# A written order for ScalarE, VectorE and GpSimd in the memory and attention stage, shorter steps in its chains, and rotations on VectorE

## The chip, the cores and the metric

The kernel runs on one core of a Trainium2 chip. The engines of the core are TensorE (PE in the rows, with PEld for its weight loads), VectorE (DVE), ScalarE (ACT), GpSimd (POOL) and SyncE (SP), whose queue issues the transfers. The metric is the device time of one execution in microseconds; lower is better. A change of less than 0.2% is about what a measurement of this kernel cannot tell from none.

## The reference

One encoder layer: 512 tokens of 2048 channels, float32. A combined projection feeds four mixers of 512 channels each; their outputs are normed, concatenated and projected back; cross attention on 256 memory tokens and a mixture of 32 experts follow. Cut to what the changed stage computes:

```python
z = rms_norm(h, norm_mix) @ w_in                  # columns split into za, zb, zc, zd
# A, diff_attention(za): 4 heads, two softmax maps of 64 channels each
q, k = apply_rope(q, cos, sin), apply_rope(k, cos, sin)
lam = exp(sum(lf[0] * lf[1])) - exp(sum(lf[2] * lf[3])) + lam_init
sc = einsum('bhcqd,bhckd->bhcqk', q, k) * scale
p = softmax(sc); attn = p[:, :, 0] - lam * p[:, :, 1]
o = rms_norm(attn @ v, subln_g) * (1 - lam_init)
# C, dilated_attention(zc): 4 heads of 128 channels, rope, keys in three strided windows
# D, s5_bidir(zd): complex linear recurrence over the sequence, both directions,
y = C x + d_skip * u;  gl = gelu(y);  od = rms_norm(gl * sigmoid(gl @ glu_w + glu_b))
h = h + concat(oa, ob, oc, od) @ w_out
# cross attention: keys and values of the memory, 4 heads of 512 channels
k, v = split(rms_norm(mem) @ wkv);  p = softmax((rms_norm(h) @ wq) k^T);  h = h + (p v) @ wo
def apply_rope(x, cos, sin):
    x1, x2 = split(x)
    return concat([x1 * cos - x2 * sin, x2 * cos + x1 * sin])
```

## The kernel before

The kernel is a sequence of stages on one instruction stream per engine. **The stage of the change** runs from about 737 to 1335 us. TensorE has one steady load there, a list of *units* (class `Units`), and two *chains* are laid into it.

The units are the memory's part of cross attention, which needs no token yet (`cross_fold`). `project` makes 128 channels of the memory's keys or values, `keys` multiplies keys by a strip of `xa_wq`, and `values` multiplies values by a strip of `xa_wo`. Every float32 product is made of three float32r products of a high and a low part (`mm3`; `split` makes the parts: the high one is a cast on ScalarE, the low one a subtraction on VectorE). So each half of a weight tile, `wraw` from memory, becomes `whi` by ScalarE and `wlo` by VectorE before TensorE can use it. `Units.get` keeps at most three halves split ahead of TensorE (`NB = 4`). A half feeds 12 matmuls of 256 columns, or 6 of 512. The names in the rows: `mh`, `ml` are the memory's parts, `kvz`, `kvh`, `kvl` a projected strip and its parts, `kvo` an output strip, `pj` the accumulators.

The chains are Python generators: `s5()` (mixer D: `s5_states`, `s5_outputs`, `s5_gate`) and `attention()` (four heads of `diff_head`, four of `dil_head`, then `norm_512`). A `yield x` says that the chain's next piece should come x microseconds of modelled TensorE time later, and `Units.step` emits pieces of units until then (x is stretched by `SLACK`: 1.5 for attention, 1.43 for s5). When the units have run out, the chain's pieces follow each other directly.

A head begins in `head_inputs`: `rope_load` fetches q and k (`at_q`, `at_k`) and copies of them with swapped halves (`at_qr`, `at_kr`), `rope` multiplies each by a table, adds the two (`at_full`) and splits the sum (`at_qh`, `at_ql`). Then come the transposition of v, and four tiles of 128 queries, each with scores (`mm3`), softmax, and a transposition one tile later.

On TensorE the order of the code is kept in this stage. On ScalarE, VectorE and GpSimd a scheduler orders the instructions, with a raised priority for the splits (`high_priority(HP)`). Each engine runs its list strictly in order, and so does each DMA queue. In the rows the program's `s5_` is written `s_`, and numbers at the end of names are left out.

## Time and profile before

| | us |
|---|---|
| runs of the kernel | 2723.89, 2726.25, 2730.3 (median 2726.25) |
| the profiled execution | 2721.49 |
| its span in the trace | 2719.8 |
| TensorE busy over the span | 2610.1 (96%) |
| VectorE, ScalarE, GpSimd busy | 1344.8 (49%), 927.9 (34%), 239.7 (9%) |

The profiled execution's time is the span and 1.7 us around it, and it lies 4.8 us below the median of the runs. TensorE is busy nearly throughout, so the rows to look for are the few in which it stands idle, with the engine that released it in brackets.

### The profile page before, as it was taken

To read this page: it belongs to the slowest core of one execution; us is meant where nothing else is said; L and a number is where in the kernel's file an instruction comes from. 1 tells how busy PE (TensorE), PEld (TensorE's weight loads), DVE (VectorE), ACT (ScalarE), POOL (GpSimd) and SP (SyncE) were. 2 spreads that over 40 slices of the span, in tenths; PEclk is the share of its full clock that TensorE was granted. 3 is DMA by queue.
4 is the path that set the end of the run, shared out by engine and by line. 5 is a ranking of instruction groups with operands and counts; after the bars stand their busy time and mean duration, and the time that the engine had idled before them with its cause. 6 is when DMAs were issued, how large, how long until landed. Compare 5 with 4: busy or idle time off the path is not lost. (4 is left out here: it accounts for less than half of the span.)

```text
span 2719.8 us, 43651 instructions
## 1 busy us (share of the span) xinstructions
PE 2610.1 (96%) x17976; PEld 1796.1 (66%) x17976; DVE 1344.8 (49%) x2407; ACT 927.9 (34%) x1695; POOL 239.7 (9%) x373
## 2 busy tenths in 40 slices
PE   8899999999979889999999999899999999999996
PEld 6787777777768778869788878644444444444432
DVE  6747474737387654566533344443334433333322
ACT  5134243443256554555533334321111111111103
POOL 0400000000024950000000000000000000000002
PEclk9999999999989989999999999899999999999999
DMA  7432121222266657756633352399999999999997
GB/s 253 163 130 69 57 75 53 88 66 72 95 173 180 200 178 217 231 178 189 229 120 121 98 186 70 152 379 423 423 423 422 425 420 424 426 424 425 421 427 305
DMA packets 156668, 639.96 MB, mean 235 GB/s; under 512 B 25264, under 2 KB 58672, under 8 KB 131376
## 3 DMA queue, kind: packets, MB, share of 16 engines
q1 hardware_dynamic: 156464, 637.12, 62.7%
q8 instruction: 143, 2.34, 0.3%
q14 instruction: 61, 0.50, 0.1%
HBM read 597.75 MB, written 39.32 MB: 234 GB/s over the span
## 5 line engine op out<-in xcount | busy, mean ns | idle before, releaser
L1035 DVE TENSOR_TENSOR wlo<-wraw,whi 128x512 fp32r<-128x512 f32 x556 | 396.1, 720 | 380.5 <-ACT whi L1034 372.2
L1034 ACT CAST whi<-wraw 128x512 fp32r<-128x512 f32 x556 | 339.4, 620 | 555.8 <-PE pj L159 480.4
L159 PE MATMUL ph<-wch,mo_xT 128*64 128x512 f32 x2048 | 455.0, 596 | 5.0 <-DMA wch<-in_moe_w_dram 4.9
L159 PEld LDWEIGHTS ph<-wch,mo_xT 128*64 128x64 f32 x2048 | 140.9, 137 | 277.2 <-issue 263.6
L159 PE MATMUL pj<-xh,whi 128*128 128x512 f32 x688 | 292.8, 426 | 7.0 <-ACT xh L1037 6.6
L159 PE MATMUL pj<-xh,wlo 128*128 128x512 f32 x688 | 272.0, 395 | 7.4 <-DVE wlo L1035 7.4
L159 PE MATMUL pj<-xl,whi 128*128 128x512 f32 x688 | 271.6, 395 | 0.0
L159 PE MATMUL py<-wch,mo_h 128*64 128x512 f32 (+1 forms) x1040 | 231.2, 591 | 2.0 <-ACT mo_h L2108 1.4
L2117 DVE TENSOR_TENSOR mo_A<-ps,mo_A 128x512 f32<-128x512 f32 (+1 forms) x260 | 163.6, 676 | 131.2 <-PE ps L2116 131.2
L1035 DVE TENSOR_TENSOR mo_lo<-H,mo_hi 128x512 fp32r<-128x512 f32 x128 | 87.8, 687 | 171.7 <-ACT mo_hi L1034 171.6
L159 PE MATMUL pj<-mh,whi 128*128 128x256 f32 x512 | 151.7, 296 | 19.3 <-ACT mh L1037 14.7
L159 PEld LDWEIGHTS pj<-xh,whi 128*128 128x128 f32 x688 | 130.4, 190 | 47.2 <-issue 10.3
L1034 ACT CAST mo_hi<-H 128x512 fp32r<-128x512 f32 x128 | 79.1, 619 | 239.5 <-PE ps L159 239.5
L159 PEld LDWEIGHTS py<-wch,mo_h 128*64 128x64 f32 x1040 | 70.7, 136 | 134.1 <-issue 115.5
L159 PEld LDWEIGHTS pj<-xh,wlo 128*128 128x128 f32 x688 | 130.4, 190 | 38.0 <-DVE wlo L1035 9.6
L159 PEld LDWEIGHTS pj<-xl,whi 128*128 128x128 f32 x688 | 130.6, 190 | 26.9 <-issue 3.1
L159 PE MATMUL pj<-mh,wlo 128*128 128x256 f32 x512 | 146.8, 287 | 0.8 <-DVE wlo L1035 0.7
L159 PE MATMUL pj<-ml,whi 128*128 128x256 f32 x512 | 146.8, 287 | 0.1
L159 PE MATMUL ps<-mo_OH,mo_hi 128*128 128x256 f32 x512 | 134.6, 299 | 5.7 <-DVE mo_OH L1997 4.8
L1037 ACT ACTIVATE mo_yh<-py,mo_g 128x512 fp32r<-128x512 f32 (+1 forms) x65 | 44.3, 681 | 246.8 <-PE py L159 246.8
L159 PE MATMUL ps<-mo_OH,mo_lo 128*128 128x256 f32 x512 | 128.3, 286 | 0.0
L159 PEld LDWEIGHTS ps<-mo_OH,mo_hi 128*128 128x128 f32 x512 | 98.9, 193 | 33.5 <-issue 32.6
(507 smaller groups left out, 4698.1 us busy)
## 6 DMA issues: line engine op xcount, KB each, us to landing
wch<-in_moe_w_dram SPq DMA_DIRECT2D x191, 2048.0 KB, 12.4
wraw<-in_w_in_dram SPq DMA_DIRECT2D x85, 512.0 KB, 3.9
wraw<-in_xa_wkv_dram SPq DMA_DIRECT2D x64, 512.0 KB, 4.6
wraw<-in_xa_wq_dram SPq DMA_DIRECT2D x32, 512.0 KB, 4.1
wraw<-in_xa_wo_dram SPq DMA_DIRECT2D x32, 512.0 KB, 4.4
wraw<-in_w_out_dram SPq DMA_DIRECT2D x32, 512.0 KB, 4.2
Ad<-kvo SPq DMA_DIRECT2D x32, 256.0 KB, 3.2
VWd<-kvo SPq DMA_DIRECT2D x32, 256.0 KB, 4.4
```

Source lines behind the costliest of these rows:

```text
L159: nc.tensor.matmul(out, lhsT, rhs, start=start, stop=stop)
L1034: nc.scalar.copy(hi, x)
L1035: nc.vector.tensor_tensor(lo, x, hi.bitcast(F32), op=OP.subtract)
L1037: nc.scalar.activation(hi, x, AF.Copy, scale=scale)
L2117: nc.vector.tensor_tensor(A[:, t, c:c + n], pc, A[:, t, c:c + n], op=OP.add)
```

## The change

Four things change in this stage; the computation stays the same.

- `units.drive(s5(), attention())` stands inside `tc.manual_schedule` for ScalarE, VectorE and GpSimd, so their instructions keep the order of the code.
- The multiplication by the second table in `rope` goes from GpSimd to VectorE.
- The chains yield more often and at other places. The eight loads of `s5_U` are issued by GpSimd's queue, not SP's. `lamv` and `lamp` get tiles of their own.
- `cross_fold` projects keys and values of a head together (8 `project` units), then runs 8 `keys` and 4 `values` units.

```diff
@@ -566,7 +566,7 @@
 def rope(k, pool, zz, tab, name):
     nc = k.nc
     a, b = zz
-    nc.gpsimd.tensor_tensor(b, b, tab[:, 1], op=OP.mult)
+    nc.vector.tensor_tensor(b, b, tab[:, 1], op=OP.mult)
     nc.vector.tensor_tensor(a, a, tab[:, 0], op=OP.mult)
     full = pool.tile([P, SEQ], F32, name="at_full")
     nc.vector.tensor_tensor(full, a, b, op=OP.add)
@@ -596,16 +596,21 @@
 
 def attn_consts(k, cp):
 
+
     nc = k.nc
     rope_table(k, cp, "ropea")
     k.biasc = cp.tile([P, 4, SEQ], F32, name="biasc")
     nc.sync.dma_start(k.biasc, k.I["c_biasc"].rearrange("(t p) s -> p t s", p=P))
+    src = k.I["diff_lambda"]
+    k.lamv = cp.tile([P, 4, 64], F32, name="lamv")
+    nc.sync.dma_start(k.lamv, bass.AP(tensor=src.tensor, offset=src.offset, ap=[[0, P], [64, 4], [1, 64]]))
+
+
+def attn_factors(k, cp):
+    nc = k.nc
     k.lam_init = 0.8 - 0.6 * math.exp(-0.3 * 0)
-    src = k.I["diff_lambda"]
-    lv = cp.tile([P, 4, 64], F32, name="lamv", tag="at_o")
-    nc.sync.dma_start(lv, bass.AP(tensor=src.tensor, offset=src.offset, ap=[[0, P], [64, 4], [1, 64]]))
-    pr = cp.tile([P, 2, 64], F32, name="lamp", tag="at_v")
-    lvv = lv.rearrange("p (a b) c -> p a b c", b=2)
+    pr = cp.tile([P, 2, 64], F32, name="lamp")
+    lvv = k.lamv.rearrange("p (a b) c -> p a b c", b=2)
     nc.vector.tensor_tensor(pr, lvv[:, :, 0, :], lvv[:, :, 1, :], op=OP.mult)
     sm = cp.tile([P, 2], F32, name="lams")
     nc.vector.tensor_reduce(sm, pr, axis=AX.X, op=OP.add)
@@ -624,11 +629,17 @@
     k.nc.scalar.copy(aT[:, :, t * P:t * P + P], pt)
 
 
-def head_inputs(k, h, pool, zT, half, tab):
-    q = rope(k, pool, rope_load(k, pool, zT, h * P, half, "at_q"), tab, "at_q")
-    kk = rope(k, pool, rope_load(k, pool, zT, 512 + h * P, half, "at_k"), tab, "at_k")
+def head_inputs(k, h, pool, zT, half, tab, us):
+
+    zq = rope_load(k, pool, zT, h * P, half, "at_q")
+    zk = rope_load(k, pool, zT, 512 + h * P, half, "at_k")
     zv = pool.tile([P, SEQ], F32, name="at_v")
     k.nc.sync.dma_start(zv, zT[1024 + h * P:1024 + h * P + P, :])
+    yield us
+    q = rope(k, pool, zq, tab, "at_q")
+    yield 0.7
+    kk = rope(k, pool, zk, tab, "at_k")
+    yield 2
     return q, kk, zv
 
 
@@ -636,8 +647,9 @@
 
     nc = k.nc
     wait = lambda us: us * SLACK["at"]
-    q, kk, zv = head_inputs(k, h, pool, zT, 32, k.ropea)
-    yield wait(6) if h else S_LOADS
+    q, kk, zv = yield from head_inputs(k, h, pool, zT, 32, k.ropea, wait(4) if h else S_LOADS - 4)
+    if h == 0:
+        attn_factors(k, pool)
     vt = token_major(k, pool, ps, zv, "at_vt")
     aT = pool.tile([P, 4, SEQ], F32, name="at_aT")
     scale = 64 ** -0.5
@@ -650,6 +662,7 @@
             cs = slice(c * 64, c * 64 + 64)
             sc.append(ps.tile([P, SEQ], F32, name="ps"))
             mm3(nc, sc[c], q[0][cs, t * P:t * P + P], q[1][cs, t * P:t * P + P], kk[0][cs], kk[1][cs], True, True)
+        yield wait(0.6)
         for c in range(2):
             s = sc[c]
             nc.vector.tensor_reduce(st[:, c:c + 1], s, axis=AX.X, op=OP.max)
@@ -657,15 +670,16 @@
             p = pool.tile([P, SEQ], F32, name=f"at_p{c}", bufs=2 - c)
             nc.scalar.activation(p, s, AF.Exp, bias=st[:, c:c + 1], scale=scale, accum_out=st[:, 2 + c:3 + c])
             pr.append(p)
+            yield wait(0.7)
         nc.vector.reciprocal(st[:, 2:4], st[:, 2:4])
         nc.vector.tensor_tensor(st[:, 3:4], st[:, 3:4], k.nlam, op=OP.mult)
         nc.vector.tensor_scalar(pr[0], pr[0], st[:, 2:3], None, op0=OP.mult)
         nc.vector.scalar_tensor_tensor(pr[0], pr[1], st[:, 3:4], pr[0], op0=OP.mult, op1=OP.add)
         if last is not None:
-            yield wait(2.5)
+            yield wait(1)
             transposed(k, ps, last, aT, t - 1)
         last = pr[0]
-        yield wait(3)
+        yield wait(2.5)
     yield wait(2)
     transposed(k, ps, last, aT, 3)
     yield wait(1.2)
@@ -686,8 +700,7 @@
 
     nc = k.nc
     wait = lambda us: us * SLACK["at"]
-    q, kk, zv = head_inputs(k, h, pool, zT, 64, k.ropec)
-    yield wait(6)
+    q, kk, zv = yield from head_inputs(k, h, pool, zT, 64, k.ropec, wait(4))
     vt = token_major(k, pool, ps, zv, "at_vt")
     aT = pool.tile([P, 4, SEQ], F32, name="at_aT")
     scale = 128 ** -0.5
@@ -697,16 +710,18 @@
         s = ps.tile([P, SEQ], F32, name="ps")
         mm3(nc, s, q[0][:, t * P:t * P + P], q[1][:, t * P:t * P + P], kk[0], kk[1], True, True)
         p = pool.tile([P, SEQ], F32, name="at_p0", bufs=2)
+        yield wait(0.4)
         nc.vector.scalar_tensor_tensor(p, s, scale, k.biasc[:, t, :], op0=OP.mult, op1=OP.add)
         nc.vector.tensor_reduce(st[:, 0:1], p, axis=AX.X, op=OP.max, negate=True)
         nc.scalar.activation(p, p, AF.Exp, bias=st[:, 0:1], accum_out=st[:, 1:2])
+        yield wait(1.2)
         nc.vector.reciprocal(st[:, 1:2], st[:, 1:2])
         nc.vector.tensor_scalar(p, p, st[:, 1:2], None, op0=OP.mult)
         if last is not None:
-            yield wait(1)
+            yield wait(0.5)
             transposed(k, ps, last, aT, t - 1)
         last = p
-        yield wait(2.5)
+        yield wait(1.5)
     yield wait(1.5)
     transposed(k, ps, last, aT, 3)
     yield wait(1.2)
@@ -868,7 +883,7 @@
     nc.sync.dma_start(k.s5_Kd[:, 576:1088], PF.rearrange("p a b t g -> p (a b t g)"))
 
 
-def s5_cmul(k, tmp, ore, oim, w, x, n, sign):
+def s5_cmul(k, tmp, ore, oim, w, x, n, sign, later=False):
 
     nc = k.nc
     t = [tmp.tile([P, 4, n, 16], F32, name=f"s5_t{i}", tag=f"s5_t{i}") for i in range(4)]
@@ -877,6 +892,8 @@
     nc.vector.tensor_tensor(ore, t[0], t[1], op=OP.subtract)
     nc.gpsimd.tensor_tensor(t[2], w(0), x(1), op=OP.mult)
     nc.gpsimd.tensor_tensor(t[3], w(1), x(0), op=OP.mult)
+    if later:
+        return lambda: nc.vector.tensor_tensor(oim, t[2], t[3], op=OP.add)
     if sign > 0:
         nc.vector.tensor_tensor(oim, t[2], t[3], op=OP.add)
     else:
@@ -897,15 +914,18 @@
     U = k.s5_U = pool.tile([P, 32, NCH], F32, name="s5_U")
     src = ud.rearrange("(g c) (t m) -> t c g m", c=16, m=NCH)
     for t in range(TC):
-        nc.sync.dma_start(U[t * 16:t * 16 + 16], src[t])
+        nc.gpsimd.dma_start(U[t * 16:t * 16 + 16], src[t])
     X = k.s5_X = pool.tile([P, 2, NCH, 2, 16], F32, name="s5_X")
+    yield wait(S_LOADS - 4)
     for d in range(2):
         for g0 in range(0, 16, 4):
             BP = tmp.tile([P, 2, 4, 8, 16], F32, name="s5_BP")
             w = lambda p: bc(PF[:, p, d, :, g0:g0 + 4].rearrange("p t g -> p g t")[:, :, :, None], [P, 4, 8, 16])
             x = lambda p: bc(Bt[:, p, g0:g0 + 4][:, :, None, :], [P, 4, 8, 16])
-            s5_cmul(k, tmp, BP[:, 0], BP[:, 1], w, x, 8, 1.0)
-            yield wait(S_LOADS if d + g0 == 0 else 1.5)
+            done = s5_cmul(k, tmp, BP[:, 0], BP[:, 1], w, x, 8, 1.0, later=True)
+            yield wait(2.5)
+            done()
+            yield wait(0.8)
             px = ps.tile([P, 2, 4, NCH], F32, name="ps")
             for p in range(2):
                 pt = ps.tile([P, 4, P], F32, name="ps")
@@ -992,6 +1012,7 @@
     nc.sync.dma_start(ut, ud.rearrange("(j p) s -> p j s", p=P))
     W = tmp.tile([P, 4, SEQ], F32, name="s5_glu")
     nc.sync.dma_start(W, I["s5_glu_w"].rearrange("l (j p) c -> p (l j) c", p=P))
+    yield wait(8)
     for j in range(4):
         nc.vector.scalar_tensor_tensor(yt[:, j], ut[:, j], vec(k, "s5_d", j), yt[:, j], op0=OP.mult, op1=OP.add)
     nc.scalar.activation(yt, yt, AF.Gelu_apprx_tanh)
@@ -999,7 +1020,7 @@
     a = k.vi["s5_glu_b"]
     nc.vector.tensor_scalar(bh, k.V[:, a:a + 4], 0.5, None, op0=OP.mult)
     gt = tmp.tile([P, 4, SEQ], F32, name="s5_gt", tag="s5_ut")
-    yield wait(18)
+    yield wait(8)
     for o in range(4):
         pg = ps.tile([P, SEQ], F32, name="ps")
         for j in range(4):
@@ -1281,13 +1302,10 @@
         return Unit(proj_rows(k, wo, None, None, 2, None).pieces, run)
 
     for h in range(4):
-        for part in range(2):
-            y = []
-            units += [project(y, part * 16 + h * 4 + j, j) for j in range(4)]
-            if part == 0:
-                units += [keys(h, d2, y) for d2 in range(8)]
-            else:
-                units += [values(h, c, y) for c in range(4)]
+        ys = [], []
+        units += [project(y, part * 16 + h * 4 + j, j) for part, y in enumerate(ys) for j in range(4)]
+        units += [keys(h, d2, ys[0]) for d2 in range(8)]
+        units += [values(h, c, ys[1]) for c in range(4)]
     return units
 
 
@@ -1534,7 +1552,8 @@
                 yield from dil_head(k, h, at, ps, zT[1536:3072], oc[h])
             yield from norm_512(k, at, ps, oc, lambda j: vec(k, "mix_out_norm", j), mixd[1024:1536, :])
 
-        units.drive(s5(), attention())
+        with tc.manual_schedule(engines={mybir.EngineType.Activation, mybir.EngineType.DVE, mybir.EngineType.Pool}):
+            units.drive(s5(), attention())
     units.finish()
     psx.close()
     psjx.close()
```

What the orders show. On SP's queue, at the start of the stage (`s5_U` is mixer D's input, `mraw` the memory, `wraw` weights), before:

```order
L900 DMA s_U<-ud 16x32x64 x8
L559 DMA at_q<-zT 128x512
L562 DMA at_qr<-zT 32x512 x4
L559 DMA at_k<-zT 128x512
L562 DMA at_kr<-zT 32x512 x4
L631 DMA at_v<-zT 128x512
L1390 DMA zT<-ev 128x512
L1464 DMA mraw<-in_memT_dram 128x512 x5
```

and of the change:

```order
L559 DMA at_q<-zT 128x512
L562 DMA at_qr<-zT 32x512 x4
L559 DMA at_k<-zT 128x512
L562 DMA at_kr<-zT 32x512 x4
L637 DMA at_v<-zT 128x512
L1408 DMA zT<-ev 128x512
L1482 DMA mraw<-in_memT_dram 128x512 x8
L1119 DMA wraw<-in_xa_wkv_dram 128x1024 x2
```

The eight loads of `s5_U` have left SP's queue, and everything behind them, `mraw` included, has moved up. On VectorE, at the beginning of the fourth head, before:

```order
L570 TENSOR_TENSOR at_k<-at_k,ropea 128x512
L1035 TENSOR_TENSOR wlo<-wraw,whi 128x512 x2
L572 TENSOR_TENSOR at_full<-at_q,at_qr 128x512
L1035 TENSOR_TENSOR wlo<-wraw,whi 128x512
L576 TENSOR_TENSOR at_ql<-at_full,at_qh 128x512
L1035 TENSOR_TENSOR wlo<-wraw,whi 128x512
L572 TENSOR_TENSOR at_full<-at_k,at_kr 128x512
L1035 TENSOR_TENSOR wlo<-wraw,whi 128x512 x2
L576 TENSOR_TENSOR at_kl<-at_full,at_kh 128x512
L1035 TENSOR_TENSOR wlo<-wraw,whi 128x512 x4
```

GpSimd has that head's first rotation among the steps of mixer D's recurrence (L942 to L945) there:

```order
L943 TENSOR_TENSOR s_s_10596<-s_A,s_X 128x64
L569 TENSOR_TENSOR at_qr<-at_qr,ropea 128x512
L944 TENSOR_TENSOR s_X<-s_X,s_s_10595 128x2x32
L945 TENSOR_TENSOR s_X<-s_X,s_s_10596 128x2x32
L942 TENSOR_TENSOR s_s_10601<-s_A,s_X 128x64
L943 TENSOR_TENSOR s_s_10602<-s_A,s_X 128x64
```

and of the change, VectorE at the beginning of the same head:

```order
L1056 TENSOR_TENSOR wlo<-wraw,whi 128x512 x4
L569 TENSOR_TENSOR at_qr<-at_qr,ropea 128x512
L570 TENSOR_TENSOR at_q<-at_q,ropea 128x512
L572 TENSOR_TENSOR at_full<-at_q,at_qr 128x512
L576 TENSOR_TENSOR at_ql<-at_full,at_qh 128x512
L569 TENSOR_TENSOR at_kr<-at_kr,ropea 128x512
L570 TENSOR_TENSOR at_k<-at_k,ropea 128x512
L572 TENSOR_TENSOR at_full<-at_k,at_kr 128x512
L576 TENSOR_TENSOR at_kl<-at_full,at_kh 128x512
L1056 TENSOR_TENSOR wlo<-wraw,whi 128x512 x4
```

The two rotations are now on VectorE, eight instructions in one block with no `wlo` among them, and GpSimd has none. On TensorE, at the end of attention, before (the last head's product with v, and what follows):

```order
L159 MATMUL ps<-at_aT,at_vt 128x512 x4
L159 MATMUL pj<-whi,kvh 128x512
L159 MATMUL pj<-wlo,kvh 128x512
L159 MATMUL pj<-whi,kvl 128x512
L159 MATMUL pj<-whi,kvh 128x512
```

and of the change (from the last unit's last three matmuls on):

```order
L159 MATMUL pj<-whi,kvh 128x512
L159 MATMUL pj<-wlo,kvh 128x512
L159 MATMUL pj<-whi,kvl 128x512
L164 MATMUL ps<-ident,at_p_15337 128x128 x4
L159 MATMUL ps<-at_kh,at_qh 128x512
L159 MATMUL ps<-at_kl,at_qh 128x512
L159 MATMUL ps<-at_kh,at_ql 128x512
L164 MATMUL ps<-ident,at_p_15404 128x128 x4
L164 MATMUL ps<-ident,at_p_15430 128x128 x4
L159 MATMUL ps<-at_aT,at_vt 128x512 x4
L159 MATMUL ps<-nm_sq,ones 128x512 x4
L159 MATMUL pj<-whi,mixh 128x512
```

Before, unit matmuls stand between the pieces of the last head and its norm, and 63 of them behind the norm's last reduction; in the change the units have run out before the last head's fourth tile, and its remaining pieces stand alone ahead of `w_out` (`pj<-whi,mixh`).

## Rows read from the trace of the kernel before

**Rows 1.** Windows by stage: length, busy (instructions) per engine, PE clock, DMA share, GB/s.

```profile
737.00:1335.00 598.00, 542.55 (x3814) 468.72 (x3812) 373.44 (x652) 335.23 (x640) 157.79 (x284) 0.96 0.66 196
...
1740.00:2720.00 980.00, 953.16 (x4792) 438.57 (x4792) 361.55 (x594) 170.19 (x291) 15.80 (x13) 0.99 0.97 406
```

**Rows 2.** Timeline of PE: start, duration, instruction, [idle before it <- releaser].

```profile
765.66 0.58 PE L159 MATMUL pj<-mh,whi 128*128 128x256 f32 x1 [14.67 <-ACT mh L1037]
...
802.91 0.58 PE L159 MATMUL pj<-kvh,whi 128*128 128x256 f32 x1 [2.87 <-ACT kvh L1034]
...
898.27 0.70 PE L159 MATMUL pj<-wlo,kvh 128*128 128x512 f32 x1 [5.12 <-DVE wlo L1035]
...
974.71 0.58 PE L159 MATMUL pj<-kvh,wlo 128*128 128x256 f32 x1 [10.26 <-DVE wlo L1035]
...
1150.78 0.42 PE L159 MATMUL pj<-mh,whi 128*128 128x256 f32 x1 [4.51 <-ACT whi L1034]
...
1335.04 0.59 PE L159 MATMUL pj<-whi,mixh 128*128 128x512 f32 x1 [2.83 <-ACT mixh L1034]
```

**Rows 3.** Narrow windows around those waits and one without, columns as in rows 1.

```profile
737.00:765.00 28.00, 13.99 (x62) 11.26 (x60) 18.09 (x32) 4.34 (x8) 8.97 (x6) 0.82 0.98 231
...
800.00:810.00 10.00, 6.49 (x41) 5.82 (x41) 5.30 (x14) 4.54 (x10) 0.29 (x1) 0.66 0.30 91
...
895.00:900.00 5.00, 1.73 (x7) 1.44 (x7) 4.25 (x5) 2.18 (x4) 4.92 (x7) 0.84 0.51 183
...
970.00:980.00 10.00, 5.29 (x24) 5.19 (x25) 4.33 (x6) 4.18 (x10) 9.37 (x19) 0.50 0.30 80
...
1050.00:1150.00 100.00, 95.92 (x808) 88.07 (x806) 43.74 (x77) 49.23 (x93) 0.00 (x0) 1.00 0.79 233
...
1335.00:1340.00 5.00, 4.96 (x15) 3.69 (x16) 1.29 (x2) 0.51 (x1) 0.00 (x0) 0.66 0.99 369
```

**Rows 4.** Timeline of DVE, the waits for GpSimd.

```profile
895.75 0.79 DVE L572 TENSOR_TENSOR at_full<-at_q,at_qr 128x512 f32<-128x512 f32 x1 [4.14 <-POOL at_qr L569]
...
973.14 0.79 DVE L572 TENSOR_TENSOR at_full<-at_q,at_qr 128x512 f32<-128x512 f32 x1 [11.16 <-POOL at_qr L569]
```

**Rows 5.** Queue of SP before the wait at 765.66: start, time on the queue.

```profile
740.72 12.56 SPq L900 DMA_DIRECT2D s_U<-ud  x8
...
760.78 2.39 SPq L1464 DMA_DIRECT2D mraw<-in_memT_dram  x5
```

**Rows 6.** Groups by line, 737 to 1340 us, on DVE and ACT.

```profile
L570 DVE TENSOR_TENSOR at_q<-at_q,ropea 128x512 f32<-128x512 f32 x4 | 2.8, 694 | 2.4 <-DMA at_q<-zT 2.4
...
L570 DVE TENSOR_TENSOR at_k<-at_k,ropea 128x512 f32<-128x512 f32 x4 | 4.8, 1206 | 3.6 <-DMA at_k<-zT 3.6
...
L572 DVE TENSOR_TENSOR at_full<-at_q,at_qr 128x512 f32<-128x512 f32 x8 | 6.7, 840 | 15.3 <-POOL at_qr L569 15.3
...
L576 DVE TENSOR_TENSOR at_ql<-at_full,at_qh 128x512 fp32r<-128x512 f32 x8 | 6.7, 834 | 0.9 <-ACT at_qh L575 0.7
...
L575 ACT CAST at_qh<-at_full 128x512 fp32r<-128x512 f32 x8 | 5.0, 619 | 48.1 <-DVE at_full L572 48.1
```

**Rows 7.** Groups by line of a dilated tile's softmax, same stretch.

```profile
L700 DVE SCALAR_TENSOR_TENSOR at_p<-ps,biasc 128x512 f32<-128x512 f32 x16 | 11.0, 688 | 8.1 <-PE ps L159 8.1
...
L702 ACT ACTIVATE at_p<-at_p,at_st 128x512 f32<-128x512 f32 x16 | 11.6, 723 | 3.3 <-DVE at_st L701 3.1
...
L704 DVE TENSOR_SCALAR at_p<-at_p,at_st 128x512 f32<-128x512 f32 x16 | 7.8, 487 | 0.6
```

**Rows 8.** Timeline of PE and ACT, the end of attention.

```profile
1206.46 4.87 PE L159 MATMUL ps<-at_aT,at_vt 128*128 128x512 f32 x8
...
1303.46 3.60 PE L159 MATMUL ps<-at_aT,at_vt 128*128 128x512 f32 x8
...
1316.11 1.28 ACT L210 ACT_TABLE_LOAD   x1 [0.97 <-PE ps L159]
...
1319.91 0.63 ACT L211 ACTIVATE nm_rs<-nm_rs 128x512 f32<-128x512 f32 x1
```

## The prediction

> **What bounds the kernel now.** I read the page first (TensorE is busy for 96% of the span), then windows by stage, TensorE's timeline for its idle places, the timelines of the engines that released it, and last the groups by line for prices. Two stages matter [rows 1]. From 1740 us on, the experts are bound by transfers: the DMA engines are 97% busy, and nothing of the change reaches them, so a microsecond won or lost earlier arrives at the end as one. The stage of the change lasts 598 us, and TensorE is busy in 542.6 of them: 55.4 us are idle. The clock is 0.96 there, so a little more is lost at the lower level. That is all that better order can win, since the change takes no work from TensorE. Six rows hold 40.3 us of it [rows 2]. The reader is to see that they have different releasers:
>
> - 14.67 us before the memory's first matmul: `mh`, ScalarE's first pass over `mraw`, comes late because SP's queue holds the eight `s_U` loads for 12.56 us ahead of the head's loads, and `mraw` is issued at 760.78 only [rows 5].
> - 5.12 and 10.26 us, released by `wlo` on VectorE. VectorE itself stood at `at_full` for 4.14 and 11.16 us, waiting for GpSimd's rotation `at_qr` [rows 4], which stands in GpSimd's list between steps of mixer D's recurrence. The `wlo` behind it waits too.
> - 2.87 us for `kvh`: four strips are projected, and `keys` wants the last at once.
> - 4.51 us for `whi` at mixer D's gate, and 2.83 us for `mixh` where `w_out` begins.
>
> After a wait the clock goes to the lower level for a while: 0.50 in the ten us around the longest rotation wait, 0.66 at 800 and at 1335 [rows 3]. I price that as the window's busy time times what is missing of the clock: 5.29 x 0.50 = 2.6 us at 970, 0.3 at 895, 2.2 at 800, 1.7 at 1335, 2.5 at 737.
>
> **The change, part by part** (minus is a gain).
>
> *A, the start.* SP's queue is free for the head's loads and `mraw` 12.6 us earlier. Bounds: with all 12.6 us and more passed on, the wait and its clock go, -14.7 - 2.5 = -17; with none, 0. Against the whole: the DMA engines are 98% busy from 737 to 765 [rows 3], so the bytes of `s_U` still compete with `mraw` when another queue issues them. And VectorE now has both rotations of head 0 in a block, behind the memory's low parts, so TensorE's next need is late as well. I take the middle, -8. `s_U` itself is covered: it is first read 33 us of TensorE time (23 x 1.43) after its loads; without that cover its 12.56 us would show.
>
> The Trainium skill, DMA: Bandwidth & Descriptors, section "Issuing engines are not separate DMA queues", says that transfers issued by different engines end on the same 16 DMA engines and interleave, so that a second issuer saves only issue time. The 98% above agrees as far as it goes. By that rule the start would give 0 in place of -8, and the sum would be -1. It is a rival below.
>
> *B, the rotations.* Removed: 5.12 + 10.26 us idle and 0.3 + 2.6 of clock, -18.3. Added: per rotation VectorE does two multiplications, the sum and the low part, with ScalarE's cast in between, in one block: 2 x 0.69 + 0.84 + 0.62 + 0.83 = 3.7 us [rows 6], for q and k 7.3 us. (The multiplication of k took 1.21 beside GpSimd; without it I take the 0.69 of q.) Behind the block wait the next `wlo` and the head's own scores. A half feeds 12 matmuls, at 95.92 / 808 = 0.119 us each about 1.4 us [rows 3], and at most three halves are split ahead, 4.3 us. So with VectorE fully ahead TensorE waits 7.3 - 4.3 = 3.0 us per head, with one half ahead 5.9, and nothing where other chain work lies beside the block or VectorE is ahead by more than the three halves of TensorE's work (chain matmuls count too). Head 0 is in A, and head 5 has the gate's matmuls beside it; six heads remain. Bounds: 0, and 6 x 5.9 = +35. I take 2 us each, +12, nearest to the full lead, since VectorE is busy only 373 of 598 us [rows 1]. Net -6 (-18 to +17).
>
> *C, eight projections together.* The last strip of the keys is now followed by four projections for the values before `keys` reads it: -2.87, and 2.2 of clock, -5 (0 if the wait returns at another strip).
>
> *D, the gate.* Its loads get 8 us before VectorE and ScalarE read them, where the in-order engines stood: -4.51 and some clock, -5. Cover is gone if the loads take longer than 11 us of TensorE time; then 0.
>
> *E, the written order and shorter steps.* Splits no longer overtake the chains' instructions. Where a cast `whi` stands behind an exponential, or a `wlo` behind a reduction, it is late by what stands ahead of it. The stage's other waits, 55.4 - 40.3 = 15.1 us, can shrink or grow by it. Lower bound: half of them go, -8. Upper: one instruction of 0.69 late in each of the 32 softmax tiles, +22. With three halves ahead most of that is covered: +4.
>
> *F, the end of attention.* In the new order the units have run out before the last head's fourth tile. Nothing lies beside its remaining pieces, which follow each other: two transpositions and three score matmuls, about 2.4 us (an estimate from the 0.4 to 0.6 us of 512-column matmuls, [rows 2]); the softmax, two instructions of 0.69, 0.72 and 0.49 [rows 7], 2.6; copy 0.6; product with v 3.6 [rows 8]; copy and square 1.2; four reductions, as many matmuls of that size, 3.6; two table loads of 1.28 and two functions of 0.63, 3.8 [rows 8]; `mixh` 0.6. Together 18.4 us, of which TensorE works 9.6; the idle 8.8 replaces the 2.83 of before: +6. The two groups of four matmuls run behind waits, and such a group took 4.87 in place of 3.60 [rows 8]: +2.5. The first two strips of `w_out` last some 5.5 us, and the third is loaded only after the norm's output has gone to memory, some 2 us too late: +2. Sum +11 (6 to 18, the upper end with a semaphore hop of 0.5 us at each of a dozen handovers).
>
> Sum: -8 - 6 - 5 - 5 + 4 + 11 = -9. Against the profiled execution's 2721.49 that is 2712; it lies 4.8 below the median of the runs, so the forecast for a median is 2726.25 - 9 = **2717 us**.
>
> **The rivals.**
>
> *Slower, by the rotation blocks.* All terms as above, but at each of the six heads VectorE is only one half ahead when it enters the block, so TensorE waits 5.9 us, +35 in place of +12: 2726 - 9 + 23 = 2740. It decides from 12 + 9 = 21 us, 3.5 per head. For it: there is not one `wlo` between the eight instructions of the fourth head, and `wlo` can't overtake any more. Against it: the stage's VectorE is idle for 225 us.
>
> *Faster, blocks hidden.* If the lead and the chains' own matmuls cover the block everywhere, B is -18: -21, 2705.
>
> *No change, stalls move.* If the written order costs a third of a microsecond per softmax tile and as much in the units, +13 in place of +4, the time stays at 2726.
>
> *The start gives nothing.* The transfers of the first 25 us are bound by the DMA engines, at 98%, not by the queue. Then A is 0 and the time 2725, no change within the bound. That is the time of the page's rule named above.
>
> **How the numbers follow.** 0.2% is 5.4 us, about what a measurement can tell here. Forecast 0.44 (its own range 2710 to 2723, so 0.37 faster and 0.07 within the bound); blocks hidden 0.10, faster; stalls move 0.09 and start gives nothing 0.05, same; rotation blocks 0.32, slower. That is 0.47 faster, 0.21 same, 0.32 slower. The range reaches from the hidden blocks with a little more of the start, 2698, to the slower rival with its tail at 18 in place of 11, cut to 2744.
>
> **What would show it.** A right: the wait for `mh` is 5 to 8 us in place of 14.67, and `mraw` is issued before 750. B right: no row of DVE waits for POOL at `at_full`, and TensorE's rows ahead of each head's first scores or of the next `wlo` show some 2 us; 4 or more at most heads is the slower rival. C and D right: no wait of over 1 us for `kvh` or at the gate. F right: 8 to 12 us idle between the last `pj<-whi,kvl` and `pj<-whi,mixh`. Wrong would make it: the score matmuls or `wlo` waiting at each softmax tile (E is then the largest term), VectorE held by `s_U`'s loads on GpSimd's queue through the `s_t` products behind them, or a tail that hides behind leftover units.

## The result and the profile after

The change makes the kernel slower: 2794.16 us in the median of 4 runs against 2725.52, ratio 1.0251 (95% interval 1.0236 to 1.0265), +69 us. The forecast was -9, and the highest time allowed for was 2744. The profiled execution has a span of 2792.3 us, 72.5 more than before, and 70.4 of them lie in the stage of the change: the first matmul of `w_out` starts at 1405.46 us, before at 1335.04 [rows 2].

Windows of the kernel after, columns as in rows 1: the stage, and its last 30 us.

```profile
737.00:1405.00 668.00, 574.00 (x3823) 479.01 (x3821) 370.40 (x671) 325.02 (x640) 125.92 (x268) 0.94 0.57 178
...
1375.00:1405.00 30.00, 12.77 (x26) 4.60 (x24) 6.41 (x12) 11.23 (x19) 0.00 (x0) 0.76 0.38 131
```

The stage has the same matmuls (3823 records to 3814), but TensorE is idle for 94 us of 668, before for 55 of 598 [rows 1], and it is busy for 31 us more with the same work. About 12 of these 31 are the clock: 0.06 x 574.0 = 34 us were missing at 0.94, 0.04 x 542.6 = 22 at 0.96 (an estimate, since the view gives the clock to two digits). The rest I put down to matmuls that follow each other less closely: the profile models their ends, so a short wait can show as busy time. No run separates that.

TensorE's timeline of the kernel after, seven of the rows with long waits.

```profile
759.36 0.58 PE L159 MATMUL pj<-mh,whi 128*128 128x256 f32 x1 [6.33 <-ACT mh L1058]
...
863.39 0.79 PE L159 MATMUL ps<-at_kh,at_qh 64*128 64x512 f32 x1 [4.74 <-ACT at_kh L575]
...
928.92 5.76 PE L159 MATMUL ps<-at_aT,at_vt 128*128 128x512 f32 x8 [6.13 <-ACT at_aT L629]
...
1032.64 0.79 PE L159 MATMUL ps<-at_kh,at_qh 64*128 64x512 f32 x1 [3.03 <-ACT at_kh L575]
...
1193.08 0.80 PE L159 MATMUL pj<-whi,kvh 128*128 128x512 f32 x1 [8.16 <-ACT whi L1055]
...
1207.96 0.79 PE L159 MATMUL pj<-whi,kvh 128*128 128x512 f32 x1 [4.90 <-ACT kvo L1294]
...
1405.46 0.80 PE L159 MATMUL pj<-whi,mixh 128*128 128x512 f32 x1 [9.60 <-ACT mixh L1055]
```

The first answers to the wait at 765.66 [rows 2], 6.33 us in place of 14.67. Those at 898 and 974 for the rotations are gone, but seven rows like the second and fourth wait for `at_kh` (16.1 us). One product with v waits 6.13 us for `at_aT`, the transposed weights of attention that ScalarE copies. The wait at the gate is now two, 8.16 and 4.90 us, and that for `mixh` 9.60 in place of 2.83. These rows do not make the 39 us of additional idleness: there were 22 waits of 0.2 us or more in the stage, now there are 75. Of them 64 are under 2 us, and they sum to 40 us; before there were 15 such short ones, with 12 us. What they wait for is mostly `whi` and `wlo`. So I looked at what ScalarE waits for.

ScalarE's waits by line in the kernel after, over the stage: total us, how often, longest.

```profile
ACT kvh L1055 <- DVE kvz L1267: 58.3, 29, 6.0
...
ACT at_p L671 <- DVE at_st L669: 47.4, 27, 4.3
...
ACT at_p L716 <- DVE at_st L715: 31.9, 16, 5.4
...
ACT whi L1055 <- DMA wraw<-in_xa_wo_dram: 20.7, 5, 10.8
...
ACT whi L1055 <- PE pj L159: 14.7, 12, 2.5
```

The same view of the kernel before.

```profile
ACT whi L1034 <- PE pj L159: 90.0, 90, 2.5
...
ACT at_p L658 <- DVE at_st L656: 13.8, 13, 3.0
...
ACT kvh L1034 <- DVE kvz L1246: 4.2, 8, 0.9
...
ACT at_p L702 <- DVE at_st L701: 3.1, 4, 1.9
```

The reader is to see the row `whi <- PE`. It is ScalarE waiting for TensorE to free a buffer of split weights, that is, being as far ahead as the buffers allow. It was 90.0 us in 90 places; now it is 14.7 in 12. ScalarE is no longer ahead, and it is not busier: it waits 58 us at `kvh` and 79 at the exponentials (`at_p`) for VectorE, before 4 and 17.

One place, ScalarE's timeline of the kernel after:

```profile
784.70 0.69 ACT L671 ACTIVATE at_p<-ps,at_st 128x512 f32<-128x512 f32 x1 [1.55 <-DVE at_st L669]
...
785.38 0.61 ACT L1055 CAST whi<-wraw 128x512 fp32r<-128x512 f32 x1
```

and TensorE's at the same place:

```profile
786.04 0.39 PE L159 MATMUL pj<-mh,whi 128*128 128x256 f32 x1 [0.66 <-ACT whi L1055]
```

ScalarE stands 1.55 us ahead of the exponential, because VectorE's maximum isn't there yet. The cast `whi` that TensorE needs stands behind that exponential, though its data are there, and TensorE waits until the cast is done.

### The profile page after: what moved, and what is told of

It reads as the page before. It is cut to its first block, busy times and chain, and to the rows that moved or that the text cites. A ratio compares the mean times of both kernels' runs of the same rounds, so it can differ in the third digit from the quotient of the medians.

```text
span 2792.3 us, 43566 instructions
## 1 busy us (share of the span) xinstructions
PE 2641.4 (95%) x17976; PEld 1806.8 (65%) x17976; DVE 1340.1 (48%) x2423; ACT 918.9 (33%) x1695; POOL 213.1 (8%) x365
## 5 line engine op out<-in xcount | busy, mean ns | idle before, releaser
L1056 DVE TENSOR_TENSOR wlo<-wraw,whi 128x512 fp32r<-128x512 f32 x556 | 386.8, 712 | 439.7 <-ACT whi L1055 409.2
L1055 ACT CAST whi<-wraw 128x512 fp32r<-128x512 f32 x556 | 332.2, 620 | 479.3 <-PE pj L159 414.0
```

The lines of the kernel that those rows point to most:

```text
L1055: nc.scalar.copy(hi, x)
L1056: nc.vector.tensor_tensor(lo, x, hi.bitcast(F32), op=OP.subtract)
```

## Experiments

Each is compared with runs of the kernel before on the same chip. Times in us are worked out from the ratio and 2725.5 where runs are compared with each other.

**1. The written order away.** The changed kernel, with one line back:

```diff
-        with tc.manual_schedule(engines={mybir.EngineType.Activation, mybir.EngineType.DVE, mybir.EngineType.Pool}):
-            units.drive(s5(), attention())
+        units.drive(s5(), attention())
```

> The changed kernel without the written order: ScalarE, VectorE and GpSimd go back to the scheduler, everything else of the change stays. Theory W (the written order: splits of weights stand behind instructions of the chains that wait, so TensorE loses its lead of split halves) expects the time to fall by most of the 69 us, to 2715 to 2740, with ScalarE's waits of whi for TensorE's buffers back near 90 us and its waits of kvh for kvz and of at_p for at_st near those of before (4 and 17 us). Theory P (the other parts: rotation blocks on VectorE, the new order of units, the uncovered end of attention) expects 2770 or more, with the waits of TensorE for at_kh (16 us) and mixh (9.6 us) unchanged.

Measured 2715.75 us, ratio 0.9972 (0.9962 to 0.9982), -8 us. The written order costs 76 us, and all the rest of the change together gives 8. ScalarE's waits in the stage:

```profile
ACT whi L1055 <- PE pj L159: 89.4, 88, 2.5
...
ACT at_p L716 <- DVE at_st L715: 11.1, 6, 6.4
...
ACT kvh L1055 <- DVE kvz L1267: 7.8, 8, 2.1
...
ACT at_p L671 <- DVE at_st L669: 5.7, 8, 1.7
```

The lead is back at 89.4 us, and the waits for VectorE are 25. Theory W holds. The window of the stage, columns as in rows 1:

```profile
737.00:1327.00 590.00, 537.80 (x3825) 463.09 (x3823) 373.88 (x671) 335.55 (x640) 142.13 (x268) 0.97 0.66 202
```

Against this run the changed kernel's stage is 78 us longer: TensorE is idle for 94 us in place of 52, and busy for 36 us more. About half of the 36 is the clock (34 us missing at 0.94, 0.03 x 537.8 = 16 at 0.97, an estimate as above).

**2. The written order alone**, on the kernel before (the same line, added).

> The kernel before with the written order alone: coarse steps, rotations on GpSimd, units and loads as before. Theory W expects it slower than before by at least as much as the change (2790 or more), since the coarse steps put whole softmax chains ahead of the splits. Theory P expects within 10 us of before, 2716 to 2736.

Measured 2872.09 us, ratio 1.0544 (1.0525 to 1.0563), +148 us. TensorE's waits, and one of VectorE's:

```profile
PE pj L159 <- ACT whi L1034: 72.8, 16, 29.7
...
PE pj L159 <- ACT kvo L1273: 66.0, 3, 64.7
...
DVE at_full L572 <- POOL at_qr L569: 58.9, 2, 57.2
```

On the kernel before the order costs 148 us, on the changed one 76. Two single waits of TensorE, 64.7 and 29.7 us, are more than the difference. Behind the longer one stands GpSimd: in the written order its rotation `at_qr` comes after mixer D's recurrence, at 1007.71 us, VectorE's `at_full` waits 57.2 us for it, and ScalarE and TensorE wait behind `at_full`. So the two runs don't show what the shorter steps are worth in the written order; with the rotations on VectorE that wait cannot come up.

**3. The moves alone**: the kernel before, scheduled, old steps, with rotations, loads and unit order of the change.

```diff
-    nc.gpsimd.tensor_tensor(b, b, tab[:, 1], op=OP.mult)
+    nc.vector.tensor_tensor(b, b, tab[:, 1], op=OP.mult)
...
-        nc.sync.dma_start(U[t * 16:t * 16 + 16], src[t])
+        nc.gpsimd.dma_start(U[t * 16:t * 16 + 16], src[t])
...
+        ys = [], []
+        units += [project(y, part * 16 + h * 4 + j, j) for part, y in enumerate(ys) for j in range(4)]
+        units += [keys(h, d2, ys[0]) for d2 in range(8)]
+        units += [values(h, c, ys[1]) for c in range(4)]
...
```

> The kernel before with the rotations on VectorE, the s_U loads on GpSimd's queue and the eight projections together, but with the scheduler and the old steps. Theory W expects a gain, 2700 to 2722: the two waits for GpSimd (18 us with the clock) and the start's 8 us go, and the scheduler lets wlo pass between the instructions of a rotation. Theory P expects 2735 or more, the rotation blocks and the unit order being the cost.

Measured 2706.44 us, ratio 0.9931 (0.9910 to 0.9952), -19 us, a version that beats both kernels. Against it, run 1 shows that the rest of the change, the shorter steps with the gate's and the end's new places and the tiles of `lamv` and `lamp`, costs 11 us once the scheduler orders the engines.

**4. The three moves one by one.** Rotations alone:

> The kernel before with the rotations on VectorE alone, scheduler, old steps, loads and units. The prediction's term B without its block cost expects -18 (the waits of 4.1 and 11.2 us at at_full and the clock behind them): 2705. If rotation work on VectorE also costs some 2 us per head with the scheduler, 2717. If the stalls move to another place, 2723.

Measured 2711.11 us, ratio 0.9953 (0.9935 to 0.9971), -13 us. TensorE's waits of that run:

```profile
PE pj L159 <- DVE wlo L1035: 7.5, 12, 1.3
```

The longest wait for `wlo` was 10.26 us [rows 2] and is 1.3; nothing waits for `at_kh`. With the scheduler, the two rotations cost VectorE's time and no wait. Eight projections together alone:

> The kernel before with the eight projections of a head together, nothing else. The prediction's term C expects -5, 2718 to 2721, and no wait of over 1 us for kvh. If the wait returns elsewhere, 2723 to 2727.

Measured 2720.20 us, ratio 0.9986 (0.9976 to 0.9997), -4 us. The wait for `kvh` is gone, but that for `mixh` is 7.14 us in place of 2.83, and TensorE is idle for 57 us in the stage, before for 55. The stage is shorter by busy time, 537 us for 543 at a clock of 0.97. The loads of `s_U` on GpSimd's queue alone:

> The kernel before with the s_U loads on GpSimd's queue alone. The prediction's term A expects -8 (bounds -17 and 0): 2715, with the wait for mh at 5 to 8 us in place of 14.7. If the DMA engines bound the start and not the queue, 2723.

Measured 2725.16 us, ratio 1.0003 (0.9994 to 1.0013): nothing. One row each of SP's queue and of TensorE, two of ScalarE, and the window of the start:

```profile
753.82 3.46 SPq L1464 DMA_DIRECT2D mraw<-in_memT_dram  x7
...
763.45 0.58 PE L159 MATMUL pj<-mh,whi 128*128 128x256 f32 x1 [12.76 <-ACT mh L1037]
...
762.37 0.62 ACT L575 CAST at_qh<-at_full 128x512 fp32r<-128x512 f32 x1 [11.19 <-DVE at_full L572]
...
762.89 0.91 ACT L1037 ACTIVATE mh<-mraw,V 128x256 fp32r<-128x256 f32 x2
...
737.00:765.00 28.00, 15.11 (x65) 12.01 (x63) 19.20 (x35) 5.42 (x11) 9.40 (x6) 0.80 0.95 308
```

`mraw` is issued 7 us earlier than in rows 5, and the first matmul starts only 2 us earlier. The DMA engines are as busy as before, 95% [rows 3], but ScalarE's rows show another reason: its list has the cast `at_qh` of head 0's rotation ahead of `mh`, and it stands there for 11.19 us. VectorE is busy without a gap from 750 to 760 us, and its `at_full` ends at 762.3. The `mh` behind it waits for no transfer. In run 3, with `mraw` issued at the same time, the scheduler had put two `mh` ahead of `at_qh`: the first began at 756.62, and TensorE waited 7.0 us. ScalarE's same rows in the kernel before:

```profile
763.78 0.62 ACT L575 CAST at_qh<-at_full 128x512 fp32r<-128x512 f32 x1 [12.31 <-DVE at_full L572]
...
765.10 0.91 ACT L1037 ACTIVATE mh<-mraw,V 128x256 fp32r<-128x256 f32 x2 [0.70 <-DMA mraw<-in_memT_dram]
```

There too `at_qh` took most of the time, and `mraw` only 0.70 us behind it. In the written order `mh` stands ahead of the rotation, and the loads matter more. Back on SP's queue there:

```diff
-        nc.gpsimd.dma_start(U[t * 16:t * 16 + 16], src[t])
+        nc.sync.dma_start(U[t * 16:t * 16 + 16], src[t])
```

> The changed kernel with the s_U loads back on SP's queue. If the queue was what made the start late, the first wait for mh grows from 6.3 back to 14 us or so and the time rises by 6 to 10 us, to 2800 to 2804. If the DMA engines bound it, the time stays within 3 us of the changed kernel's 2794.

Measured 2799.09 us, ratio 1.0279 (1.0260 to 1.0297), 8 us above the changed kernel by the ratios (5 by the medians); the two intervals overlap. The first wait for `mh` grew from 6.3 to 16.1 us, all of it for `mraw`.

**5. Which engine's order.** The changed kernel with the written order on one engine alone.

```diff
-engines={mybir.EngineType.Activation, mybir.EngineType.DVE, mybir.EngineType.Pool}
+engines={mybir.EngineType.Activation}     # w_act
+engines={mybir.EngineType.DVE}            # w_dve
```

> The changed kernel with the written order on ScalarE alone; VectorE and GpSimd by the scheduler. Theory S (ScalarE's order costs: its casts whi stand behind kvh and the exponentials, which wait for VectorE, 58 and 79 us in the changed kernel) expects most of the 78 us above the scheduled version, 2770 to 2795. Theory V (VectorE's order costs: the wlo and the rotation blocks) expects 2715 to 2740.

> The changed kernel with the written order on VectorE alone; ScalarE and GpSimd by the scheduler. Theory S expects 2715 to 2740, theory V 2770 to 2795. If each engine's order costs by itself because whi and wlo are a chain over both, both runs lie well above 2740 and each below 2794.

Measured 2755.00 us, ratio 1.0107 (1.0079 to 1.0134), and 2756.12 us, ratio 1.0115 (1.0090 to 1.0139). Neither theory S nor V: each order alone costs 37 and 39 us above run 1, and all three together 76. GpSimd's order was not run alone; the sum of the two leaves nothing for it, if they add up. TensorE's waits in the run with ScalarE's order:

```profile
PE pj L159 <- DVE wlo L1056: 23.9, 18, 4.1
```

and with VectorE's, with ScalarE's lead in that run:

```profile
PE ps L159 <- ACT at_kh L575: 17.8, 7, 4.0
...
ACT whi L1055 <- PE pj L159: 108.2, 95, 3.9
```

The wait of 17.8 us for `at_kh` belongs to VectorE's order. With ScalarE's alone, VectorE's scheduler begins the rotations earlier (13 to 59 us from a head's first `at_full` to its first scores, in the changed kernel 5 to 14), and there is no wait for `at_kh`. The two orders cost in different ways. ScalarE's takes its lead (20.8 us in the stage). VectorE's leaves that lead whole, 108.2 us, and the run is still 39 us slower than run 1: TensorE is idle for 70 us in its stage, against 52, and `at_kh` alone is as much as the difference. The rest is busy time, at a clock of 0.94.

**6. ScalarE's waits made shorter**, in the written order on all three engines. A step between maximum and exponential:

```diff
             nc.vector.tensor_scalar(st[:, c:c + 1], st[:, c:c + 1], -scale, None, op0=OP.mult)
+            yield wait(0.7)
             p = pool.tile([P, SEQ], F32, name=f"at_p{c}", bufs=2 - c)
             nc.scalar.activation(p, s, AF.Exp, bias=st[:, c:c + 1], scale=scale, accum_out=st[:, 2 + c:3 + c])
             pr.append(p)
-            yield wait(0.7)
+        yield wait(0.7)
...
```

(and the same in `dil_head`, 0.9 + 0.6 for 1.2).

> The changed kernel, written order on all three engines, with a step put between VectorE's maximum and ScalarE's exponential in each softmax tile, the steps' sum nearly as before (0.7 us more per tile of the first four heads, 0.3 of the others). Theory S expects ScalarE's waits of at_p for at_st to fall from 79 us to under 30 and the time by 10 to 30 us, to 2765 to 2785. If ScalarE's waits cost nothing by themselves (it has slack), the time stays within 5 us of 2794 or rises.

Measured 2775.92 us, ratio 1.0190 (1.0170 to 1.0209), -17 us against the change; ScalarE waits 22 us at the exponentials in place of 79. Its lead has not come back:

```profile
ACT whi L1057 <- PE pj L159: 16.0, 16, 2.1
```

The gain is smaller than what the edit did beside the units, for the added steps use the units up sooner. The last unit's matmul ends 62 us ahead of `w_out`, in the changed kernel 31, and TensorE idles for 29 us of them, there for 18. Up to the last unit it is idle for 54 us in place of 77. Then the split of a projected strip one strip later:

```diff
             nc.vector.tensor_tensor(z, pj, k.mrs, op=OP.mult)
-            split(k, y[0][j], y[1][j], z)
+            parts()
+            pend.append((y[0][j], y[1][j], z))
```

(`parts` splits what is in `pend`; `keys` calls it too, ahead of its first matmul.)

> The changed kernel, written order, with a projected strip's split (kvh, kvl) put one strip later than its kvz, so that ScalarE does not stand at kvh for VectorE. If these waits of ScalarE delay the casts whi behind them, its waits of kvh for kvz fall from 58 us to under 15 and the time by 8 to 20 us, to 2774 to 2786. If there is slack behind them, the time stays within 5 us of 2794.

Measured 2780.32 us, ratio 1.0198 (1.0181 to 1.0215), -14 us; the waits at `kvh` fell from 58.3 to 5.7 us.

**7. The rotation blocks cut**, written order: a bare `yield` in `rope` after the first product, after the sum and after the high part, each 0.9 us in `head_inputs`.

> The changed kernel, written order, with the rotation of q and of k each cut into four steps of 0.9 us, so that wlo and kvz can stand between them. If the undivided blocks cost what the prediction's term B says (12 us; the trace after shows 15 us of waits for at_kh at six heads), TensorE's waits for at_kh fall under 5 us and the time by 10 to 20 us, to 2774 to 2784. If the steps only move the waits to whi and wlo, or lengthen the chains past the units' end, the time stays at 2790 or more.

Measured 2786.17 us, ratio 1.0221 (1.0204 to 1.0238), -8 us, which is at the edge of the noise (the intervals touch). The last matmul of the units, and TensorE's waits:

```profile
1334.44 0.39 PE L159 MATMUL pj<-whi,kvl 128*128 128x512 f32 x1
...
PE ps L159 <- ACT at_kh L577: 5.1, 2, 4.1
...
PE pj L159 <- ACT whi L1066: 30.1, 20, 7.3
...
PE ps L164 <- DVE at_p L730: 10.8, 8, 2.5
```

Less than expected. `at_kh` fell from 16.1 to 5.1 us, but `whi` rose from 19.5 to 30.1 and the transpositions' wait for `at_p` from 4.1 to 10.8. The first row says where: all the waits for `at_kh` and `at_p` come after 1334 us, when the units have run out. That is 67 us ahead of `w_out`, in the changed kernel 31, so the whole last head stands alone, and TensorE idles there for 31 us in place of 18. While units lasted, no wait for `at_kh` was left, and TensorE was idle for 60 us in place of 77. So the cut did what it was meant to do, and a part of its gain was lost to the longer uncovered end; the rise of `whi` is another part.

**8. The end covered**, written order: `"at": 1.5` to `1.3` in `SLACK`.

> The changed kernel with attention's waits stretched by 1.3 in place of 1.5, so that 48 unit matmuls lie between the last head's product and the norm's last reduction and 102 behind it, where there were none. If the uncovered end costs what the prediction's term F says (11 us; the trace after shows 17 us of waits from the last unit to w_out, and matmuls at the lower clock besides), the time falls by 11 to 25 us, to 2769 to 2783, and the wait for mixh falls from 9.6 to under 4 us. If denser chains cost as much in waits for whi and wlo as the end gives back, the time stays within 5 us of 2794.

Measured 2777.95 us, ratio 1.0196 (1.0177 to 1.0214), -15 us against the change. TensorE's waits:

```profile
PE pj L159 <- ACT mixh L1055: 1.7, 1, 1.7
...
PE pj L159 <- ACT whi L1055: 25.2, 21, 4.8
```

The wait for `mixh` fell from 9.60 to 1.7 us, and those for `whi` and `at_kh` rose by 6 and 4.

**9. Together**: 6 with both edits, and `"at": 1.1`.

> The changed kernel, written order, with the later exponential and the later kvh together, and attention's waits stretched by 1.1, so that 120 unit matmuls lie behind the norm's last reduction. If the pieces add up, the later exponential gives 18, the covered end 16 and the later kvh 8 to 20: 2740 to 2752. If they hide behind each other, 2760 or more. The scheduled version's 2716 is reached only if nothing else in the written order costs.

Measured 2736.17 us, ratio 1.0039 (1.0026 to 1.0052), -58 us against the change, where the parts alone gave 17 + 14 + 15 = 46. The parts are not quite the same, for run 8 had 1.3; and with 1.1 units last to the end here, which takes from run 6 its longer uncovered end. ScalarE's waits in the stage:

```profile
ACT whi L1057 <- PE pj L159: 38.8, 30, 2.9
...
ACT at_p L718 <- DVE at_st L716: 23.9, 12, 4.3
...
ACT at_p L672 <- DVE at_st L669: 23.7, 18, 2.6
...
ACT kvh L1057 <- DVE kvz L1275: 5.6, 4, 2.8
```

The lead is back to 38.8 us. The time is still 18 us above the scheduled version of run 1, with the rotation blocks left as they are.

**10. The best version**: run 3, a step of 8 us behind the gate's loads (the later one 10 in place of 18), and `"at": 1.45`.

> The moves without the written order (rotations on VectorE, s_U on GpSimd's queue, eight projections together; 2706), and besides a step of 8 us between the gate's loads and their first use, and attention's waits stretched by 1.45 in place of 1.5, so that 150 unit matmuls lie behind the norm's last reduction in place of 69. Expected: the wait of 7.4 us for mixh falls to under 3, and the time to 2698 to 2704. If the wait for mixh stays, it is the loads of the mixers' outputs that are late, and the time is 2704 to 2708.

Measured 2696.77 us, ratio 0.9893 (0.9876 to 0.9910), -29 us. TensorE's waits at its two ends:

```profile
PE pj L159 <- ACT mh L1038: 7.6, 1, 7.6
...
PE pj L159 <- DVE ml L1039: 5.6, 2, 5.1
...
PE pj L159 <- ACT mixh L1035: 1.7, 1, 1.7
```

The wait for `mixh` is 1.7 us; the start still waits for 13.

## Why the prediction was wrong

*The step that failed is E, the written order: +4, with +22 as its upper bound.* It measured +76. I priced an instruction that stands in the way by its duration, 0.69 us in 32 tiles (16 of them have two exponentials). What a strictly ordered engine loses is the time that the instruction in front waits, and these waits were 137 us on ScalarE alone (58 at `kvh`, 79 at the exponentials). They are not spent beside the lead of three halves, as I took it: ScalarE's lead is made by running ahead, and it is gone (90 to 15 us). Run 1 shows that the order is the cause: without it 76 us come back, and the lead with them. Runs 6 and 9 show that ScalarE's waits are a part of it: shortened, they give 17 and 14, and 58 with the end covered. Run 5 shows that it is not one engine's fault. But the lead is no measure of the time. Run 6 gained 17 us with the lead at 16, and VectorE's order alone loses 39 us with the lead whole: there the rotation blocks, which I had in B, are what TensorE waits for. How the slower clock and the many short waits for `whi` and `wlo` divide the rest was not separated.

*B, net -6.* The removal was right in kind: -18 forecast, -13 measured alone. The block was priced at 2 us for each of six heads; the rows for `at_kh` show 15 us at six heads. But the block belongs to VectorE's written order: scheduled, the same instructions cost nothing. Cutting the blocks took away every wait for `at_kh` beside the units, and gave 8 us net.

*A, -8.* Alone 0, and my reading of the wait was wrong. I had put the 14.67 us down to SP's queue. ScalarE's rows of the kernel before show that it stood 12.31 us at `at_qh`, and 0.70 more for `mraw`, so an earlier `mraw` could not bring much. The rival "the start gives nothing" had the right time for the move alone, but not the reason: it was ScalarE's order behind VectorE's work, not the 95% of the DMA engines. Where `mh` stands ahead of the rotation, the move took the wait from 16.1 to 6.3 us, with the DMA engines still 96% busy. The Trainium skill's page DMA: Bandwidth & Descriptors, "Issuing engines are not separate DMA queues", leaves a second issuer the issue time, and the trace agrees that far, with `mraw` issued 7 us earlier. That the start would give 0 does not follow from it, for the issue time on SP's queue was 12.56 us.

*C, -5.* The time was right, -4 alone, and in the profile after TensorE has no wait for `kvh`. The sum was not: in the run alone `mixh` took back more than `kvh` gave, and the gain lies in busy time. So the agreement is in part luck.

*D, -5.* Wrong in the trace: the wait of 4.51 us at the gate became 8.16 and 4.90. Ahead of the first, ScalarE waited 10.8 us for weights of `xa_wo`, while the DMA engines were fully busy (a DMA share of 1.04 in the view from 1185 to 1190 us); the gate's three loads and a head's inputs are issued there too. The scheduled run 1 shows the same wait with 8.2 us, so it isn't the written order's. No run moved the gate's loads alone; that they crowd out the weights is argued, not shown.

*F, +11.* Right in kind and short in size: I had 8.8 us of idleness after the last unit, the trace shows 18, and covering the end gave 15. Rows of TensorE, SP and ScalarE at the end of the kernel after:

```profile
1373.75 0.40 PE L159 MATMUL pj<-whi,kvl 128*128 128x512 f32 x1
...
1381.60 6.40 PE L159 MATMUL ps<-at_aT,at_vt 128*128 128x512 f32 x8 [0.68 <-ACT at_aT L629]
...
1394.74 1.13 PE L159 MATMUL ps<-nm_sq,ones 128*128 128x512 f32 x2 [0.72 <-ACT nm_sq L740]
...
1401.93 12.38 SPq L1601 DMA_DIRECT2D mixr<-mixd  x10
...
1404.79 0.62 ACT L1055 CAST mixh<-mixr 128x512 fp32r<-128x512 f32 x1 [6.17 <-DMA mixr<-mixd]
```

The product with v took 6.40 us at the lower clock in place of 3.60 [rows 8], the four reductions went one by one with ScalarE's squares, and ScalarE's first `mixh` stood 6.17 us until after the loads that SP issued at 1401.93, behind the norm's stores. I had put 2 us there, counting on two strips loaded earlier; why they did not serve is not shown. For the upper end of 18 I had taken 0.5 us at each handover. That figure rests on no row of these runs, and the handover that can be read here is far shorter: ScalarE's last square ends at 1394.68, and TensorE's reduction of it starts at 1394.74.

*The rivals.* The slower one, rotation blocks at 2740, named a cost that exists, but its 16.1 us are a fifth of the 76. What I had listed as making the prediction wrong, E as the largest term, is what came, though TensorE's rows name `whi` (19.5 us) as well as `wlo` (14.9). That the forecast of -9 is near what the rest of the change gives, -8 without the written order, is chance: the forecast's terms without E sum to -13, and the single moves give -13, -4 and 0, of which the shorter steps, the gate and the uncovered end take part back.

*Open.* Of the 76 us, 58 were regained in run 9, the cover of the end among them, which isn't the written order's alone (run 1 also waits 9.5 us for `mixh`). What makes the remaining 18 us above run 1 was not separated; 18.3 us of waits for `at_kh` stand in that run, and no run has the cut blocks of run 7 together with a covered end.

## What to carry to other kernels

Before an engine's order is written by hand, look for the row in which a supplying engine waits for its consumer's buffers: it is that engine's lead, and if it is large, the scheduler is letting supplies overtake waiting work. Do it for each engine on the way, since one engine's lead says nothing of the next one's. Price an in-order instruction by how long it will stand, not by how long it takes, and put a step between a producer on one engine and its consumer on the next. Steps use up the filler work sooner, so look where the filler ends before you judge them. When a wait is put down to a transfer, look at what the waiting engine did just before it. Try moves of work and of loads apart from the order: here the moves were worth 19 us, 29 with a step at the gate and the end covered, and the order lost 76.

## What was not expected of the hardware

Stalls cost more than their idle rows: with the same matmuls, TensorE's busy time grew by 31 us, of which the lower clock explains about 12. Of the 39 us more idleness 28 came from waits of under 2 us, which no list of the longest waits shows.
